# The head of a mixer reordered: x times its norm early, adaLN sums as columns on TensorE, h^T written ahead of the filter norms

## The chip, the cores and the metric

One of the cores of a Trainium2 chip runs the whole program. The metric is the device time of one execution in microseconds (us). The kernel before has a median of 2262.38 us over 3 runs (2261.64 to 2263.37). One more execution was taken by the hardware profiler; the views quoted here are of that one.

The engines are called as in the profile: PE (TensorE, matmul) with PEld (its weight loads), DVE (VectorE), ACT (ScalarE), POOL (GpSimd), SP (the queue that issues most DMAs).

## The reference, cut to what matters

The program is one encoder block on x (1024 tokens of 1024 channels, float32): a mixer (a Hyena branch with long convolutions, and attention) and 16 experts. What the change touches is the beginning of the mixer:

```python
h = RMSNorm(x)*(1+scale1)+shift1        # scale1, shift1: columns of silu(c) @ w_ada + b_ada
z = h @ w_in                            # 34 blocks of 128 columns

# the filters of the Hyena branch
hdn = jnp.sin(fr[0] * (z @ w1 + b1))
hdn = jnp.sin(fr[1] * (hdn @ w2 + b2))
hdn = jnp.sin(fr[2] * (hdn @ w3 + b3))
h = (hdn @ w4).reshape(L, HY_ORDER, 2, HY_WIDTH)
h = h * jnp.exp(-t01[:, :, None, None] * jnp.abs(deltas))
h = h / (jnp.sum(jnp.abs(h), axis=0, keepdims=True) + EPS)
```

In the filter part z is a table of time features, and h is the filters; in the first two lines h is the normed x. w_ada gives six groups of 1024 columns; the head needs the first two, the shift and the scale.

## The kernel before, in words

Nearly all products are made to float32 accuracy from three matmuls of split operands (`mm3`, L143 to L146: high by high, high by low, low by high). An operand is split by a copy to a shorter format on ACT and a subtraction on DVE (`wsplit`, L136; the `wl` and `wh` tiles). A projection block of w_in is 1024 by 128, its tile `wr` of 512 KB comes from a ring of two buffers (`wload`, L131).

The program is `mixer_head`, then `attention`, `merge`, `project`, `choose`, `experts`. The change lies in `mixer_head`. It computes, for x transposed to channels by tokens (`xt`, eight tiles of 128 by 1024):

- the filter network: three layers of 66, 128 and 64 inputs (L237, L309), each followed by `sine` (range reduction on DVE, L223 to L229) and `sin` on ACT. The results, split, are `Hs`.
- the sum of x² over the channels: ACT squares a tile (L254), PE multiplies it with a column of ones (L256; row form: the ones are a one-column weight, the square moves 512 columns at a time, and all eight k add up in PSUM). `columns()` turns the row into columns by two ACT copies (L244) and eight one-column matmuls (L247). `rsqrt` (L148) makes r, eight transposes (L334) spread it over all partitions, and ACT copies that to `rb` (L335).
- the scale group of adaLN: of its eight weight tiles `stage[1][k]`, four are scaled on ACT (L315, L317) and added on POOL (L318), four more are accumulated by `adaln` on DVE (L157 to L162) into `acc`, and `mod_cols` (L164) sums over the partitions with eight one-column matmuls (L167). G1 is (1 + scale) times the norm's gain.
- the shift group: row form on PE (L342, `stage[0][k]` moving 512 columns at a time), then `columns()`.
- h^T: DVE makes x times G1 times rb (L349), ACT adds the shift and rounds to `hTh` (L358), DVE makes the rest `hTl` (L359).
- the filter norms: `norms(o)`, o = 0 and 1, is a generator. Each multiplies split w4 with `Hs` (L271, L272), takes Abs on ACT (L274), multiplies with the decay (L266) and sums on DVE (L275), eight times; then it scales w4 by 1/norm. Four steps of norms(0) stand in front of h^T, the rest behind it, then norms(1).

Behind that come: the spectra of the filters (a plane of filter values is made by `filt_plane`, L415; its matmul is L420 and L421), transforms by `fft8` on DVE, the blocks 12 to 17 of w_in (q, k, v), the blocks 0 to 11 (Hyena's inputs), the two convolutions, and the blocks 18 to 33 (gates). The gates' blocks have the lowest priority (`lane(2)`): they fill PE where nothing else is ready.

A scheduler that works ahead of time fixes the order on each engine from the order of the program, priorities and its own estimates of time. Inside `in_order()` (L113) PE, ACT and DVE keep the written order among themselves; the head from the first sine to h^T stands in such a block. SP issues the DMAs in one sequence, and a DMA waits for the one issued eight before it.

Of the kernel before, what the change touches and what calls it, by code (L numbers as in the profile page):

```python
# [51 lines left out]
def block(tc, xT, cols_d, rows_d, mlp_d, w4_d, dfc_d, idf_d, rope_d, wada_d, win_d, why_d, watt_d, wout_d, wr_d,  # L52
          wg_d, wu_d, wd_d, out, dbg=None, upto=99):
    nc = tc.nc
# [127 lines left out]
    def mixer_head():  # L182
# [11 lines left out]
        def z4(shape=(128, 1024), dt=F32):  # L194
            return wk.tile(list(shape), dt, name="z4", tag="z4", bufs=3)
# [19 lines left out]
        nc.sync.dma_start(delb, row("del"))  # L215

# [20 lines left out]
            mm(ps, mcol(w, parts), h, start=True, stop=True)  # L237
            return ps

        def columns(row):  # L240

            t = z4([1, 1024])
            for hf in range(2):
                nc.scalar.copy(t[:, hf * 512:hf * 512 + 512], row[hf])  # L244
            ps = pM([128, 8])
# [4 lines left out]
        sums = [pT([1, 512]) for hf in range(2)]  # L250

        def square(k):
            sq = z4()
            nc.scalar.activation(sq, xt[k], AF.Square)  # L254
            for hf in range(2):
                mm(sums[hf], ones[:, 0:1], sq[:, hf * 512:hf * 512 + 512], start=k == 0, stop=k == 7)  # L256

        w4s = []

        def norms(o):  # L260
            raw = w4r[o]
            w4h, w4l = wsplit(raw)
            yield
            for b in range(4):
                dec = wk.tile([128, 1024], F32, name="dec", tag="Z", bufs=4)
                nc.scalar.activation(dec, t01b, AF.Exp, scale=col("ndel", b))  # L266
                for dr in range(2):
                    m = dr * 4 + b
                    ps = pS()
                    for hf in range(2):  # L270
                        mm(ps[:, hf], w4h[:, m * 128:(m + 1) * 128], Hs[hf], start=True, stop=False)  # L271
                        mm(ps[:, hf], w4l[:, m * 128:(m + 1) * 128], Hs[hf], start=False, stop=True)  # L272
                    t = f4([128, 1024])
                    nc.scalar.activation(t, ps.rearrange("p a b -> p (a b)"), AF.Abs)  # L274
                    nc.vector.scalar_tensor_tensor(t, t, 1.0, dec, op0=ALU.mult, op1=ALU.mult,  # L275
                                                   accum_out=rn[:, o * 8 + m:o * 8 + m + 1])
                    yield
# [15 lines left out]
        Hs = []  # L293
        with in_order():
            h = sine(layer("w1", mcol("z", 66), 66), "b1", "f1")
            for k in range(3):
                square(k)
            sin(h)
            ps = layer("w2", h)
            for k in range(3, 7):  # L300
                square(k)
            h = sine(ps, "b2", "f2")
            sin(h)
            square(7)
# [5 lines left out]
            n0 = norms(0)  # L310
            next(n0)
            hs = [sine(t, "b3", "f3") for t in ps]
            pv = columns(sums)
            acc, w = z4(), stage[1]
            nc.scalar.activation(acc, w[0], AF.Copy, scale=siluc[:, 0:1])  # L315
            for k in range(1, 4):
                nc.scalar.activation(w[k], w[k], AF.Copy, scale=siluc[:, k:k + 1])  # L317
                nc.gpsimd.tensor_add(acc, acc, w[k])  # L318
                if k > 1:
                    s = hs[k - 2]  # L320
                    sin(s)
                    t = hsp.tile([128, 512], F32R, name=f"Hs{len(Hs)}")
                    nc.scalar.copy(t, s)
                    nc.vector.tensor_sub(t[64:128], s[64:128], t[64:128])
                    Hs.append(t)
# [3 lines left out]
            rb = w2("H", [128, 1024])  # L329
            for hf in range(2):  # L330
                ps = pM()
                for j in range(4):
                    q = hf * 4 + j
                    nc.tensor.transpose(ps[:, j * 128:j * 128 + 128], rr[:, q:q + 1].to_broadcast([128, 128]), ident)  # L334
                nc.scalar.copy(rb[:, hf * 512:hf * 512 + 512], ps)  # L335
            for k in range(4, 8):
                adaln(acc, w[k], k)
            prow = [pT([1, 512]) for hf in range(2)]

            def shift(k):  # L340
                for hf in range(2):
                    mm(prow[hf], siluc[:, k:k + 1], stage[0][k][:, hf * 512:hf * 512 + 512], start=k == 0, stop=k == 7)  # L342
            for k in range(4):
                next(n0)
                shift(k)
            mod_cols(acc, 1, pM)
            nc.vector.scalar_tensor_tensor(G1, modc[:, 8:16], 1.0, col("g_mix", 0, 8), op0=ALU.add, op1=ALU.mult)
            for k in range(8):
                nc.vector.scalar_tensor_tensor(xt[k], xt[k], G1[:, k:k + 1], rb, op0=ALU.mult, op1=ALU.mult)  # L349
                if k < 4:  # L350
                    shift(k + 4)
            nc.vector.tensor_add(modc[:, 0:8], columns(prow), col("b_ada", 0, 8))
            sx.close()
            hpool = hx.enter_context(tc.tile_pool(name="hT", bufs=1, side="right", reuse_waits="tile"))
            hTh, hTl = [[hpool.tile([128, 1024], F32R, name=f"hT{i}{k}") for k in range(8)] for i in range(2)]
            for k in range(8):
                u, b = xt[k], modc[:, k:k + 1]
                nc.scalar.activation(hTh[k], u, AF.Identity, bias=b)  # L358
                nc.vector.scalar_tensor_tensor(hTl[k], u, b, hTh[k], op0=ALU.add, op1=ALU.subtract)  # L359
        for _ in n0:  # L360
            pass
        if "Hs" in dbg:
            for hf in range(2):
                nc.sync.dma_start(dbg["Hs"][hf], Hs[hf].bitcast(F32))
# [2 lines left out]
                nc.sync.dma_start(dbg["hT"][0, k], hTh[k].bitcast(F32))  # L367
                nc.sync.dma_start(dbg["hT"][1, k], hTl[k].bitcast(F32))

        for _ in norms(1):  # L370
            pass


        def win_block(m, evac, n=0):
            raw = wload(win_d[m])
            wh, wl = wsplit(raw)
            for hf in range(2):
                sl = slice(hf * 512, hf * 512 + 512)
                ps = pM()
                with lane(n) if n else ExitStack():  # L380
                    for k in range(8):
                        ks = slice(k * 128, k * 128 + 128)
                        mm3(ps, (wh[:, ks], wl[:, ks]), (hTh[k][:, sl], hTl[k][:, sl]), k == 0, k == 7)
                evac(ps, sl)

        def hyena_in(m, n=0):
# [1054 lines left out]
```

## Time and profile before

| | us |
|---|---|
| median of 3 runs | 2262.38 |
| lowest, highest | 2261.64, 2263.37 |
| the profiled execution | 2259.1 |
| its span on the core | 2257.3 |
| PE busy, of the span | 2126.8 (94%) |
| DVE busy | 1905.6 (84%) |
| ACT busy | 1310.2 (58%) |
| POOL busy | 126.3 (6%) |

How to read the views: times count from the start of the span. A windows row gives a stretch (from:to and its length), the busy time and count of instructions of PE, PEld, DVE, ACT and POOL, then PEclk (the clock that TensorE was granted, 1.00 is full), the share of the DMA engines and GB/s. A timeline row is start, length, engine, line, operation, output tile and inputs, partitions x elements, how many instructions in a row; in brackets the idle time ahead of it and what ended it. A group's row is line, engine, operation, tiles, count, then busy time in us and mean ns of one, then idle time before and its releasers. A matmul of float32 operands is carried out as more than one pass and leaves more than one record.

### The profile page before, as it was taken

Reading aid. Unit: us, or ns where it says so; the run is one execution under the profiler, and the core shown is the slowest. Engines: PE = TensorE matmul, PEld = TensorE weight load, DVE = VectorE, ACT = ScalarE, POOL = GpSimd, SP = SyncE. Lnnn points to the kernel's source line nnn. Section 1 sums busy time; section 2 is a strip of 40 time slices with the busy share of each in tenths; the row PEclk is TensorE's granted clock in tenths of the full one; section 3 lists DMA queues with packets and bytes.
Section 4 is the critical chain, followed back from the end, with each engine's and each line's share of the span. In section 5 each row is a group of like instructions: output and inputs, shape, how many; then the busy total and the mean of one; then the engine's idle time right before and its main releaser. Section 6 shows DMA issues by size and latency. Waiting matters only on the chain. (4 is left out here: it accounts for less than half of the span.)

```text
span 2257.3 us, 26834 instructions
## 1 busy us (share of the span) xinstructions
PE 2126.8 (94%) x10076; PEld 1682.6 (75%) x10076; DVE 1905.6 (84%) x2150; ACT 1310.2 (58%) x1424; POOL 126.3 (6%) x130
## 2 busy tenths in 40 slices
PE   5799999999979999998699999999999999999997
PEld 1487887878768887775577777777778777787776
DVE  6888897998968888644789988898998989889986
ACT  5654453242367774213477766677677677677675
POOL 1011000010000000002100010000000000000000
PEclk8899999999989999998899999999999999999999
DMA  7046755554442224667699999999999999999984
GB/s 281 21 142 201 289 205 168 172 155 153 144 145 94 66 66 143 212 226 278 222 361 369 364 363 321 377 368 375 363 355 377 371 375 360 359 377 365 380 323 149
DMA packets 138134, 588.87 MB, mean 261 GB/s; under 512 B 13714, under 2 KB 34450, under 8 KB 88724
## 3 DMA queue, kind: packets, MB, share of 16 engines
q1 hardware_dynamic: 122308, 546.25, 64.6%
q0 software_dynamic: 15696, 40.90, 7.0%
q8 instruction: 79, 1.29, 0.2%
q14 instruction: 51, 0.42, 0.1%
HBM read 530.48 MB, written 56.62 MB: 260 GB/s over the span
## 5 line engine op out<-in xcount | busy, mean ns | idle before, releaser
L1161 DVE TENSOR_TENSOR el<-raw,eh 128x2048 fp32r<-128x2048 f32 (+1 forms) x451 | 861.6, 1947 | 61.2 <-ACT eh L1160 58.5
L1160 ACT CAST eh<-raw 128x2048 fp32r<-128x2048 f32 (+1 forms) x456 | 721.6, 1642 | 58.2 <-PE py L146 29.8
L145 PE MATMUL pM<-el,xh 128*128 128x512 f32 x1024 | 405.4, 396 | 8.7 <-DVE el L1161 8.6
L144 PE MATMUL pM<-eh,xh 128*128 128x512 f32 x1024 | 405.8, 396 | 7.9 <-ACT eh L1160 6.1
L146 PE MATMUL pM<-eh,xl 128*128 128x512 f32 x1024 | 400.9, 392 | 0.0
L145 PEld LDWEIGHTS pM<-el,xh 128*128 128x128 f32 x1024 | 192.3, 188 | 62.0 <-DVE el L1161 24.1
L144 PEld LDWEIGHTS pM<-eh,xh 128*128 128x128 f32 x1024 | 192.2, 188 | 50.3 <-ACT eh L1160 8.9
L146 PEld LDWEIGHTS pM<-eh,xl 128*128 128x128 f32 x1024 | 192.3, 188 | 37.7
L144 PE MATMUL pM<-hT,wh 128*128 128x512 f32 x544 | 214.2, 394 | 4.8 <-ACT wh L139 3.7
L146 PE MATMUL pM<-hT,wl 128*128 128x512 f32 x544 | 212.9, 392 | 0.6 <-DVE wl L140 0.6
L145 PE MATMUL pM<-hT,wh 128*128 128x512 f32 x544 | 213.2, 392 | 0.0
L145 PE MATMUL py<-el,hh 128*128 128x512 f32 x512 | 205.2, 401 | 1.4 <-DVE el L1161 1.3
L144 PE MATMUL py<-eh,hh 128*128 128x512 f32 x512 | 201.8, 394 | 1.8 <-ACT hh L1236 1.5
L146 PE MATMUL py<-eh,hl 128*128 128x512 f32 x512 | 200.6, 392 | 0.0
L139 ACT CAST wh<-wr 128x1024 fp32r<-128x1024 f32 (+1 forms) x60 | 56.2, 936 | 162.5 <-PE pM L145 83.4
L144 PEld LDWEIGHTS pM<-hT,wh 128*128 128x128 f32 x544 | 102.6, 189 | 26.1 <-ACT wh L139 4.1
L146 PEld LDWEIGHTS pM<-hT,wl 128*128 128x128 f32 x544 | 102.3, 188 | 22.2 <-DVE wl L140 1.3
L145 PEld LDWEIGHTS pM<-hT,wh 128*128 128x128 f32 x544 | 102.6, 189 | 20.9
L144 PEld LDWEIGHTS py<-eh,hh 128*128 128x128 f32 x512 | 96.5, 188 | 26.2 <-ACT hh L1236 6.0
L145 PEld LDWEIGHTS py<-el,hh 128*128 128x128 f32 x512 | 96.4, 188 | 24.0 <-DVE el L1161 4.7
L146 PEld LDWEIGHTS py<-eh,hl 128*128 128x128 f32 x512 | 96.6, 189 | 19.1 <-DVE hl L1237 0.4
L1224 ACT ACTIVATE hd<-pM 128x512 f32<-128x512 f32 x64 | 38.3, 598 | 113.2 <-PE pM L146 113.0
(368 smaller groups left out, 3467.2 us busy)
## 6 DMA issues: line engine op xcount, KB each, us to landing
raw<-in_wg_dram SPq DMA_DIRECT2D x128, 1024.0 KB, 7.1
raw<-in_wu_dram SPq DMA_DIRECT2D x128, 1024.0 KB, 6.9
raw<-in_wd_dram SPq DMA_DIRECT2D x128, 1024.0 KB, 7.4
wr<-in_win_dram SPq DMA_DIRECT2D x34, 512.0 KB, 3.7
dc<-in_dfc_dram POOLq DMA_DIRECT2D x48, 256.0 KB, 2.9
wr<-in_wada_dram SPq DMA_DIRECT2D x24, 512.0 KB, 3.8
st<-in_wada_dram SPq DMA_DIRECT2D x16, 512.0 KB, 10.0
H<-H_s SPq DMA_DIRECT2D x16, 512.0 KB, 3.8
```

Of the source, the lines that this page charges most:

```text
L139: nc.scalar.copy(h, raw)
L144: mm(o, a[0], b[0], start=start, stop=False)
L145: mm(o, a[0], b[1], start=False, stop=False)
L146: mm(o, a[1], b[0], start=False, stop=stop)
L1160: nc.scalar.copy(h[:, ks], raw[:, ks])
L1161: eng.tensor_sub(l[:, ks], raw[:, ks], h[:, ks])
L1224: nc.scalar.activation(hd, ps2[0], AF.Silu)
```

## The change

- Order of the loads: before mlp, x, w4[0], t01, scale weights, w4[1], shift weights, del. After: mlp, x, scale weights, shift weights, the block 12 of w_in, w4[0], t01, w4[1], del. The w4 tiles leave the ring `wr` for buffers of their own.
- x²: the first two squares are summed by column groups (`by_columns`: the tile's eight 128 by 128 pieces are the weights, a column of ones moves), the other six are added on DVE into `total`, which is then summed by one group into the same eight PSUM columns. `columns()` goes.
- rb stays in PSUM, and x is multiplied by it at once, between the steps of `adaln` on the first four scale tiles.
- The scale: `acc` (four tiles, DVE) by a column group, and four more groups with the other tiles as weights and silu(c) as the moving column. No ACT scaling, no POOL addition.
- The shift: eight column groups instead of the row form.
- h^T: x times G1 plus shift, on ACT for odd k and on DVE for even k; a cast on ACT gives `hTh`, a subtraction on DVE `hTl`.
- `norms` is a plain function now; both calls stand behind h^T, outside the block that keeps the written order.
- The block 12 of w_in is loaded and split in the head, and its two halves run together, k by k.

```diff
-        w4r = [wload(w4_d[0])]
+        for i in (1, 0):
+            for k in range(8):
+                nc.sync.dma_start(stage[i][k], wada_d[i, k])
+        first = wload(win_d[12])
+        w4r = [w2("X", [128, 1024]) for o in range(2)]
+        nc.sync.dma_start(w4r[0], w4_d[0])
         t01b = w2("H", [128, 1024])
         nc.sync.dma_start(t01b, row("t01"))
-        for k in range(8):
-            nc.sync.dma_start(stage[1][k], wada_d[1, k])
-        w4r.append(wload(w4_d[1]))
-        for k in range(8):
-            nc.sync.dma_start(stage[0][k], wada_d[0, k])
+        nc.sync.dma_start(w4r[1], w4_d[1])
...
-        def columns(row):
...
+        def by_columns(ps, w, v, start, stop):
+
             for m in range(8):
-                mm(ps[:, m:m + 1], t[:, m * 128:(m + 1) * 128], ones[0:1, 0:1], start=True, stop=True)
-            return ps
+                mm(ps[:, m:m + 1], w[:, m * 128:(m + 1) * 128], v, start=start and m == 0, stop=stop and m == 7,
+                   skip_group_check=True)
...
             h = sine(layer("w1", mcol("z", 66), 66), "b1", "f1")
-            for k in range(3):
-                square(k)
+            pv = pT([128, 8])
+            for k in range(2):
+                by_columns(pv, square(k), ones[:, 0:1], k == 0, False)
             sin(h)
             ps = layer("w2", h)
-            for k in range(3, 7):
-                square(k)
+            total = zt()
+            nc.vector.tensor_add(total, square(2), square(3))
             h = sine(ps, "b2", "f2")
+            sq = square(4)
+            nc.vector.tensor_add(total, total, sq)
             sin(h)
...
+            for k in range(5, 8):
+                nc.vector.tensor_add(total, total, square(k))
+            by_columns(pv, total, ones[:, 0:1], False, True)
...
-            acc, w = z4(), stage[1]
-            nc.scalar.activation(acc, w[0], AF.Copy, scale=siluc[:, 0:1])
-            for k in range(1, 4):
-                nc.scalar.activation(w[k], w[k], AF.Copy, scale=siluc[:, k:k + 1])
-                nc.gpsimd.tensor_add(acc, acc, w[k])
...
+            acc = zt()
+            for k in range(4):
+                adaln(acc, stage[1][k], k)
+                for i in (2 * k, 2 * k + 1):
+                    nc.vector.tensor_mul(xt[i], xt[i], rb.rearrange("p a b -> p (a b)"))
+            pg = pM([128, 8])
+            by_columns(pg, acc, ones[:, 0:1], True, False)
+            for k in range(4, 8):
+                by_columns(pg, stage[1][k], siluc[:, k:k + 1], False, k == 7)
...
-            for k in range(4):
-                next(n0)
-                shift(k)
-            mod_cols(acc, 1, pM)
...
+            pg = pM([128, 8])
             for k in range(8):
-                nc.vector.scalar_tensor_tensor(xt[k], xt[k], G1[:, k:k + 1], rb, op0=ALU.mult, op1=ALU.mult)
-                if k < 4:
-                    shift(k + 4)
-            nc.vector.tensor_add(modc[:, 0:8], columns(prow), col("b_ada", 0, 8))
+                by_columns(pg, stage[0][k], siluc[:, k:k + 1], k == 0, k == 7)
+            first = wsplit(first)
+            nc.vector.tensor_add(modc[:, 0:8], pg, col("b_ada", 0, 8))
...
-            for k in range(8):
-                u, b = xt[k], modc[:, k:k + 1]
-                nc.scalar.activation(hTh[k], u, AF.Identity, bias=b)
-                nc.vector.scalar_tensor_tensor(hTl[k], u, b, hTh[k], op0=ALU.add, op1=ALU.subtract)
-        for _ in n0:
-            pass
+
+            def shifted(k):
+                if k % 2:
+                    nc.scalar.activation(xt[k], xt[k], AF.Identity, scale=G1[:, k:k + 1], bias=modc[:, k:k + 1])
+                else:
+                    nc.vector.tensor_scalar(xt[k], xt[k], G1[:, k:k + 1], modc[:, k:k + 1], op0=ALU.mult, op1=ALU.add)
+
+            shifted(0)
+            for k in range(0, 8, 2):
+                nc.scalar.copy(hTh[k], xt[k])
...
+        norms(0)
...
-        for _ in norms(1):
-            pass
+        norms(1)
```

What this does to the order on the engines. PE before, at the end of the adaLN sums: the last column group of the scale (`z_262` is acc), the last rows of the shift (`st_106` to `st_109` are the weights' tiles), and the turn into columns:

```order
L167 MATMUL pM<-ones,z_262 128x1 [waits DVE_49]
L167 MATMUL pM<-ones,z_262 128x1 x7
L342 MATMUL pT<-st_106,siluc 1x512 [waits DMAHW1_49]
L342 MATMUL pT<-st_106,siluc 1x512
L342 MATMUL pT<-st_107,siluc 1x512 [waits DMAHW2_49]
L342 MATMUL pT<-st_107,siluc 1x512
L342 MATMUL pT<-st_108,siluc 1x512 [waits DMAHW3_49]
L342 MATMUL pT<-st_108,siluc 1x512
L342 MATMUL pT<-st_109,siluc 1x512 [waits DMAHW4_49]
L342 MATMUL pT<-st_109,siluc 1x512
L247 MATMUL pM<-ones,z_375 128x1 [waits Activation_49]
L247 MATMUL pM<-ones,z_375 128x1 x3
```

PE after, at the end of the same sums: the last two of the eight shift groups, and then the filter norms' first matmuls (`z_455` and `z_456` are the split w4, `Hs_333` and `Hs_335` the network's result):

```order
L244 MATMUL pM<-siluc,st_108 128x1 [waits DMAHW0_49]
L244 MATMUL pM<-siluc,st_108 128x1 x7
L244 MATMUL pM<-siluc,st_109 128x1 [waits DMAHW1_49]
L244 MATMUL pM<-siluc,st_109 128x1 x7
L269 MATMUL pS<-Hs_333,z_455 128x512 [waits DVE_49,Activation_49]
L270 MATMUL pS<-Hs_333,z_456 128x512
L269 MATMUL pS<-Hs_333,z_455 128x512 [waits PE_49]
L269 MATMUL pS<-Hs_335,z_455 128x512 [waits DVE_49]
L270 MATMUL pS<-Hs_335,z_456 128x512
L270 MATMUL pS<-Hs_333,z_456 128x512
L269 MATMUL pS<-Hs_335,z_455 128x512
L270 MATMUL pS<-Hs_335,z_456 128x512
```

The sums that were matmuls of 512 moving columns are matmuls of one moving column now, eight for each weight tile, and no norm matmul stands between them any more.

ACT before, where h^T begins (`f_126` to `f_128` are x's tiles, `f_343` and `f_431` the norms'):

```order
L423 ACTIVATE wn<-delb,cols 128x512 [waits DMAHW5_49]
L274 ACTIVATE f_343<-pS 128x1024 [waits DVE_49,PE_49]
L244 COPY z_375<-pT 1x512 [waits PE_49] x2
L274 ACTIVATE f_431<-pS 128x1024 [waits DVE_49,PE_49]
L358 ACTIVATE hT_392<-f_126,modc 128x1024 [waits DVE_49]
L358 ACTIVATE hT_393<-f_127,modc 128x1024 [waits DMAHW6_49]
L358 ACTIVATE hT_394<-f_128,modc 128x1024 [waits DMAHW7_49]
```

ACT after, at the same place (`f_466` and `f_474` are the norms', `X` the raw w4):

```order
L264 ACTIVATE dec<-H,cols 128x1024 [waits DVE_49,PE_49]
L272 ACTIVATE f_466<-pS 128x1024 [waits PE_49]
L260 CAST z_549<-X 128x1024 [waits DMAHW5_49]
L357 CAST hT_415<-f_126 128x1024 [waits DVE_49]
L351 ACTIVATE f_127<-f_127,modc,G_73 128x1024
L272 ACTIVATE f_474<-pS 128x1024 [waits DVE_49,PE_49]
L359 CAST hT_416<-f_127 128x1024 [waits Activation_49]
L357 CAST hT_417<-f_128 128x1024
```

Since the norms stand outside the block that keeps the written order, the scheduler has put the first Abs and the second w4's cast ahead of h^T's first cast, and twelve norm matmuls ahead of the first projection matmul on PE.

More of the change, by code (lines that the diff above doesn't have):

```diff
@@ L254, in square, with zt @@
             nc.scalar.activation(sq, xt[k], AF.Square)
-            for hf in range(2):
-                mm(sums[hf], ones[:, 0:1], sq[:, hf * 512:hf * 512 + 512], start=k == 0, stop=k == 7)
+            return sq
+        def zt(dt=F32):
+            return wk.tile([128, 1024], dt, name="zt", tag="Z", bufs=4)
         w4s = []
@@ L261, in norms @@
             raw = w4r[o]
-            w4h, w4l = wsplit(raw)
-            yield
+            w4h, w4l = z4(dt=F32R), z4(dt=F32R)
+            nc.scalar.copy(w4h, raw)
+            nc.vector.tensor_sub(w4l, raw, w4h)
             for b in range(4):
@@ L309, in mixer_head @@
                 mm(ps[hf], mcol("w3")[pr], h[pr], start=True, stop=True)
-            n0 = norms(0)
-            next(n0)
-            hs = [sine(t, "b3", "f3") for t in ps]
-            pv = columns(sums)
-            acc, w = z4(), stage[1]
-            nc.scalar.activation(acc, w[0], AF.Copy, scale=siluc[:, 0:1])
-            for k in range(1, 4):
-                nc.scalar.activation(w[k], w[k], AF.Copy, scale=siluc[:, k:k + 1])
-                nc.gpsimd.tensor_add(acc, acc, w[k])
[L319 to L325, printed above, removed]
+            for k in range(5, 8):
+                nc.vector.tensor_add(total, total, square(k))
+            by_columns(pv, total, ones[:, 0:1], False, True)
+            h = [sine(ps[0], "b3", "f3")]
             v, rr, rt = v1, r1, rt1
@@ L340, in shift @@
-            def shift(k):
-                for hf in range(2):
-                    mm(prow[hf], siluc[:, k:k + 1], stage[0][k][:, hf * 512:hf * 512 + 512], start=k == 0, stop=k == 7)
-            for k in range(4):
-                next(n0)
-                shift(k)
-            mod_cols(acc, 1, pM)
+            rb = pS()
+            for q in range(8):
+                nc.tensor.transpose(rb[:, q // 4, q % 4 * 128:q % 4 * 128 + 128],
+                                    rr[:, q:q + 1].to_broadcast([128, 128]), ident)
@@ new lines, in mixer_head @@
+            h.append(sine(ps[1], "b3", "f3"))
+            for t in h:
+                sin(t)
+            acc = zt()
[7 more added lines that the diff above has]
+                by_columns(pg, stage[1][k], siluc[:, k:k + 1], False, k == 7)
@@ L347, in mixer_head @@
+            for hf in range(2):
+                t = hsp.tile([128, 512], F32R, name=f"Hs{hf}")
+                nc.scalar.copy(t, h[hf])
+                Hs.append(t)
+            nc.vector.tensor_add(modc[:, 8:16], pg, col("b_ada", 8, 8))
             nc.vector.scalar_tensor_tensor(G1, modc[:, 8:16], 1.0, col("g_mix", 0, 8), op0=ALU.add, op1=ALU.mult)
+            for hf in range(2):
+                nc.vector.tensor_sub(Hs[hf][64:128], h[hf][64:128], Hs[hf][64:128])
+            pg = pM([128, 8])
@@ L368, in mixer_head, with step @@
                 nc.sync.dma_start(dbg["hT"][1, k], hTl[k].bitcast(F32))
-        for _ in norms(1):
-            pass
+        norms(1)
         def win_block(m, evac, n=0):
[L375 to L378, printed above, removed]
+            wh, wl = first if m == 12 else wsplit(wload(win_d[m]))
+            def step(ps, sl, k):
+                ks = slice(k * 128, k * 128 + 128)
+                mm3(ps, (wh[:, ks], wl[:, ks]), (hTh[k][:, sl], hTl[k][:, sl]), k == 0, k == 7)
+            halves = [slice(hf * 512, hf * 512 + 512) for hf in range(2)]
+            if m == 12:
+                ps = [pM() for sl in halves]
+                for k in range(8):
+                    for hf, sl in enumerate(halves):
+                        step(ps[hf], sl, k)
+                for hf, sl in enumerate(halves):
+                    evac(ps[hf], sl)
+                return
+            for sl in halves:
                 ps = pM()
```

25 lines of the change are left out of this document (7 added, 18 removed).

## The prediction

> **What bounds the kernel now.** I read the page's totals first, then busy time by stage, then PE's waits, then the timeline at the seams.
>
> ```profile
> span 2257.3 us, 26834 instructions
> PE 2126.8 (94%) x10076; PEld 1682.6 (75%) x10076; DVE 1905.6 (84%) x2150; ACT 1310.2 (58%) x1424; POOL 126.3 (6%) x130
> ```
>
> The windows view (busy us per engine, PEclk the granted clock) cuts the span where the head ends and where attention's tail begins:
>
> ```profile
> 12.41:43.00 30.59, 16.43 (x51) 4.74 (x49) 20.49 (x23) 15.24 (x19) 7.80 (x3) 0.78 0.97 394
> 43.00:108.00 65.00, 47.10 (x161) 26.06 (x162) 52.07 (x74) 41.10 (x45) 0.00 (x0) 0.82 0.05 17
> 108.00:370.00 262.00, 258.11 (x1179) 209.29 (x1178) 223.72 (x320) 130.30 (x187) 19.66 (x37) 1.00 0.61 203
> 370.00:607.00 237.00, 232.05 (x1042) 189.27 (x1040) 221.33 (x275) 72.93 (x94) 11.15 (x22) 1.00 0.48 149
> ```
>
> From 108 to 607 PE is busy 490.2 of 499 us: it is the bound there, and DVE has 38 and 16 us to spare in the two stages. So the head (0 to 108) is a prologue in front of a PE-bound stretch. It costs what passes until the first filter plane can be multiplied, less whatever matmuls of the projections PE gets done before, for those are missing from the stretch behind. Two times mark it: the first ACTIVATE of h^T and the first filter plane.
>
> ```profile
> 73.38 8.41 ACT L358 ACTIVATE hT<-f,modc 128x1024 fp32r<-128x1024 f32 x8
> ...
> 107.40 0.63 PE L420 MATMUL pT<-w4h,Hs 128*128 128x512 f32 x1
> ```
>
> The head's waits on PE name the chain to the first of them (us in total, times, longest):
>
> ```profile
> PE pM L334 <- DVE r L155: 15.9, 1, 15.9
> ...
> PE pS L271 <- ACT f L274: 10.8, 5, 8.0
> ```
>
> DMA doesn't bind it: it has little left to move after 40 us (DMA share 0.14 here, 0.05 above), and PE does nothing in the 10 us before.
>
> ```profile
> 30.00:40.00 10.00, 0.00 (x0) 0.00 (x0) 9.72 (x10) 2.30 (x3) 5.68 (x3) 0.50 1.02 419
> 40.00:50.00 10.00, 4.24 (x13) 2.85 (x14) 8.41 (x14) 6.49 (x9) 0.67 (x1) 0.50 0.14 49
> ```
>
> **The clock.** The granted clock decides this case, so I looked for what moves it. All its changes in this trace lie on one grid of 3.413 us. Windows on that grid, with PE's busy time and the clock:
>
> ```profile
> 60.20:63.61 3.41, 3.41 (x21) 2.20 (x21) 2.02 (x5) 0.00 (x0) 0.00 (x0) 1.00 0.00 0
> 94.33:97.75 3.42, 1.99 (x8) 1.36 (x8) 3.42 (x7) 3.42 (x5) 0.00 (x0) 1.00 0.39 134
> 101.16:104.57 3.41, 2.40 (x5) 1.47 (x6) 3.31 (x7) 0.40 (x1) 0.00 (x0) 0.50 0.00 0
> 104.57:107.99 3.42, 3.42 (x13) 3.03 (x13) 1.38 (x2) 0.43 (x1) 0.00 (x0) 0.50 0.46 158
> 1043.25:1046.66 3.41, 3.41 (x23) 2.29 (x22) 0.27 (x2) 2.19 (x4) 0.00 (x0) 1.00 0.01 2
> 1046.66:1050.07 3.41, 2.73 (x15) 2.00 (x14) 1.66 (x9) 2.33 (x4) 0.00 (x0) 0.50 0.00 0
> ```
>
> 94.33 holds only 1.99 us of 512-column matmuls, and the next window keeps 1.00. 1043.25 is busy all of its 3.41 us, and the clock falls. What fills it are matmuls that move one column:
>
> ```profile
> 1043.49 1.05 PE L974 MATMUL pT<-ones,sq 128*128 128x1 f32 x8
> ...
> 1045.43 1.05 PE L974 MATMUL pT<-ones,sq 128*128 128x1 f32 x8
> ```
>
> I take it that a one-column matmul counts for next to nothing as activity. The window at 60.20, just over half columns and the rest 512-column, kept its clock, so the threshold lies between its wide share (0.44) and the other's (a third). To rise it takes more: 2.40 us of wide matmuls (101.16) did not do it, a full window (104.57) did.
>
> The Trainium skill ("TensorE: Matmul & The Clock Gate", "Part 1: The HAM clock gate") lets the clock rise after about one busy window of 3.4 us; by it the new chain would be warm almost at once, and the time that of the first rival below. The trace's 1043.25, busy throughout and followed by 0.50, disagrees.
>
> **The price of a column group** (8 matmuls, 16 records). At full clock, L167's group takes 16 loads in 1.86 us, and PE follows the loads:
>
> ```profile
> 60.23 1.95 PE L167 MATMUL pM<-ones,z 128*128 128x1 f32 x16
> 60.23 1.86 PEld L167 LDWEIGHTS pM<-ones,z 128*128 128x128 f32 x16 [0.86 <-issue]
> 47.28 0.34 PEld L271 LDWEIGHTS pS<-Hs,wh 128*128 128x128 f32 x1
> 51.44 0.19 PEld L271 LDWEIGHTS pS<-Hs,wh 128*128 128x128 f32 x1 [0.86 <-issue]
> ```
>
> One load takes 0.34 us at clock 0.50 (47.28) and 0.19 at 1.00 (51.44). So a group is 1.86 us warm and 1.86 x 0.34/0.19 = 3.3 us cold.
>
> The same page, "LDWEIGHTS (loading the stationary operand)", gives a load by its columns alone, P/1.2 ns, with no clock in it; by that a group's 16 loads would be some 1.7 us at either clock (an estimate from that page), the second rival. The rows with 0.34 and 0.19 disagree.
>
> **The change, in order of time.** The new head gives PE no wide matmul but the filter layers until h^T, so I run its PE at half clock throughout.
>
> Its prices, from the timeline (start, us, engine, line, operation) and, for Square and the scalings, from the groups of the head (busy us, mean ns):
>
> ```profile
> 4.57 2.08 PE L237 MATMUL pM<-f 66*128 66x512 f32 x2 [4.57 <-DMA f<-in_mlp_dram]
> ...
> 6.68 0.81 DVE L223 TENSOR_SCALAR wf<-pM,cols 128x512 f32<-128x512 f32 x1 [5.61 <-PE pM L237]
> ...
> 8.45 2.14 DVE L228 SCALAR_TENSOR_TENSOR wf<-sl,wf 128x512 f32<-128x512 f32 x3
> 10.63 0.43 DVE L229 TENSOR_SCALAR wf<-wf 128x512 f32<-128x512 f32 x1
> ...
> 28.62 6.30 DVE L228 SCALAR_TENSOR_TENSOR wf<-sl,wf 128x512 f32<-128x512 f32 x3
> ...
> 45.76 1.94 PE L334 MATMUL pM<-ident,r 128*128 128x128 f32 x8 [15.94 <-DVE r L155]
> ...
> 47.88 3.92 DVE L162 SCALAR_TENSOR_TENSOR z<-st,siluc,z 128x1024 f32<-128x1024 f32 x3
> ```
>
> ```profile
> L275 DVE SCALAR_TENSOR_TENSOR f<-f,dec 128x1024 f32<-128x1024 f32 x16 | 18.9, 1224 | 6.0 <-ACT f L274 5.3 <-ACT dec L266 0.7
> ...
> L254 ACT ACTIVATE z<-f 128x1024 f32<-128x1024 f32 x8 | 8.4, 1056 | 9.2 <-DMA f<-in_xT_dram 6.5 <-PE pT L256 2.7
> ```
>
> x²: the first two squares become column groups, from 9.1 us (first layer, sine and Square before) to 9.1 + 6.6 = 15.7; layer 2 to 17.8 (2.08 cold); its sine to 22.2 (from before's first sine: its three L228 in 2.14, L229 0.43 and three steps ahead of them, 6.68 to 11.06, 4.4). The six other squares are summed on DVE; of those five adds, four lie behind the sine at 1.2 each (the price of L275, the same width): 27.2. ACT's Squares at 1.06 keep ahead. The total's group ends at 30.5. Third sine meanwhile, then v and the Newton steps to 33.2, transposes of the norm 1.94, to 35.2. Before, they ended at 47.7: x's norm is ready 12 us earlier. Part of that is the removed POOL adds: three of L228 take 2.14 us alone, 6.30 beside them.
>
> Then DVE: fourth sine to 37.6; four adaLN steps (3.92 for three, about 1 for the first) and, of the x scalings at 1.22, the six ahead of the last step: 4.9 + 7.3 = 12.2, acc ready at about 50. All weights have landed by then, so the DMA's new order costs nothing; what moved behind it (w4, t01, del) is needed only later.
>
> PE: thirteen column groups in one chain (acc, four of the scale, eight of the shift), each waiting for nothing else: 13 x 3.3 = 43 us, to 93. The shift's row form (L342) goes away. h^T then starts at 93 against 73.4: **20 us later**. x is already scaled, so h^T itself is no longer than before.
>
> Behind that ACT is the longest: by the order, five norm matmuls still stand between the chain and the first Abs (at twice the warm 0.23 of the pair below, 2.3 us). The groups of the head:
>
> ```profile
> L274 ACT ACTIVATE f<-pS 128x1024 f32<-128x1024 f32 x16 | 16.1, 1019 | 7.2 <-PE pS L272 5.9 <-DVE f L275 1.4
> ...
> L342 PE MATMUL pT<-st,siluc 128*1 128x512 f32 x32 | 14.8, 601 | 0.0
> ...
> L266 ACT ACTIVATE dec<-H,cols 128x1024 f32<-128x1024 f32 x8 | 9.0, 1148 | 0.0
> ```
>
> One pair of the projections' matmuls in the timeline:
>
> ```profile
> 109.65 0.40 PE L145 MATMUL pM<-hT,wh 128*128 128x512 f32 x1
> 109.88 0.40 PE L146 MATMUL pM<-hT,wl 128*128 128x512 f32 x1
> ```
>
> L342's 14.8 us, which go, lay partly beside DVE's work on x; what they cost is already in before's 73.4. From the first Abs to the first plane ACT has 16 Abs, eight casts of h^T, four shifts, the decays not yet made (four) and five casts of weights: 37 items at about 1.0, 37 us; with 3 us of stalls (PE cold, transposes of the norms) the first plane comes at 93 + 2.3 + 40 = 135, **28 us later** than 107.4. "h^T ahead of the filter norms" isn't quite done: one Abs and one cast stand ahead of the first cast of h^T; this lies in the sum.
>
> Given back: by the order PE now has 93 projection matmuls done ahead of the first plane, before it had 7. At the pitch of 0.23 us (109.65 to 109.88) 86 of them are 19.8 us that are missing behind 108, where PE is the bound.
>
> Sum: 28 - 19.8 = +8 us. Further on the order uses the projections up earlier (all done ahead of the last 28 token transposes, before of the last 16), so some filler is missing at the end of the PE-bound stretch; I add 1. 2259.1 (the profiled execution, span 2257.3) + 9 = 2268.1; the three runs' median, 2262.38, lies 3.3 above the profiled time: 2271.4, so **2272**. The unknown costs: the column group between 2.9 and 3.6 (5 us either way over 13), stalls between 0 and 8: 2264 to 2280.
>
> **The rivals.**
> First, faster: columns count as activity, the chain warms within one window of its start. 13 x 1.86 + 1.7 = 26 us, h^T at 76, first plane at 76 + 1.2 + 40 = 117, +10; minus 19.8: -10, 2252. Deciding point: a group under 2.6 us (3.3 less 9/13) makes the sum negative. For it: 60.20 kept its clock; against it: 1043.25. Chance 0.13.
> Second: loads cost the same at either clock. 13 x 1.9 = 25, plane at 50 + 25 + 2.3 + 40 = 117, so 2252 to 2257 with what stays cold. Against it: 0.34 and 0.19. Chance 0.05.
> Third, slower still: DVE becomes the bound in the mixer. It has 38 us to spare from 108 to 370, and starts its transforms 28 us late with filler already spent; if half of the 19.8 us done ahead come back as PE's waits for planes, that is 10 more, 2282. For it: DVE is busy 223.7 of 262; against: it has 16 more later. Chance 0.08.
>
> **How the numbers follow.** The forecast has 0.74. Some 0.2% (4.5 us) is what a measurement of this kernel can tell. Faster than 2257.9: first rival 0.12, second 0.03, the forecast's tail 0.01: 0.16. Within: the rest of both rivals 0.03, the forecast's low end (a group at 2.9) 0.11: 0.14. Slower: 0.70. The range 2258 to 2286 leaves out the fast rivals, 0.16, and a little above, 0.03. The forecast's own is 2264 to 2280.
>
> **What would show it.** Right: granted clock 0.50 from about 13 to about 95 us; L244's thirteen groups at 3.2 to 3.4 us; first h^T cast near 93; first plane near 135; PE past 98% from there to the tail. Wrong: groups at 1.9 us or the clock at 1.00 in the chain (first rival), loads at 0.19 with the clock at 0.50 (second), PE waits for DVE's spectra after 140 us (third); an acc that is ready much before 50 would move everything earlier.

## The result and the profile after

The changed kernel takes 2291.54 us (median of 4 runs, 2288.93 to 2292.72) against 2262.88 (4 runs, 2261.64 to 2265.99): 1.0123 times as long, 95% interval 1.0105 to 1.0141. It is slower by 28.7 us, not by the 9.6 that were forecast, and lies above the range. The profiled execution's span is 2290.4, 33.1 more than before. One of the ten executions of e3_less_pe, below, took 5902.09 us, and its ratio is that of the other nine.

The head and PE-bound stretch in the windows view of the profile after:

```profile
0.00:50.00 50.00, 18.57 (x64) 13.39 (x64) 34.38 (x51) 22.26 (x25) 2.56 (x9) 1.00 0.87 338
50.00:95.00 45.00, 44.59 (x209) 44.59 (x210) 6.54 (x10) 1.15 (x1) 0.00 (x0) 1.00 0.04 12
95.00:140.00 45.00, 42.16 (x173) 31.60 (x173) 38.23 (x58) 37.62 (x40) 0.00 (x0) 1.00 0.11 41
140.00:639.00 499.00, 481.15 (x2146) 386.69 (x2146) 446.70 (x595) 201.06 (x280) 31.66 (x60) 0.99 0.53 175
```

From 50 to 95 PE does one thing, and DVE and ACT have next to nothing to do (6.54 and 1.15 of 45 us). The timeline shows what it is, and what it leads to:

```profile
50.41 3.57 PE L244 MATMUL pM<-ones,zt 128*128 128x1 f32 x16 [13.28 <-DVE zt L162]
53.84 8.46 PE L244 MATMUL pM<-siluc,st 128*128 128x1 f32 x39
```

```profile
97.32 1.02 ACT L272 ACTIVATE f<-pS 128x1024 f32<-128x1024 f32 x1 [42.16 <-PE pS L270]
98.24 1.04 ACT L260 CAST z<-X 128x1024 fp32r<-128x1024 f32 x1
99.17 1.04 ACT L357 CAST hT<-f 128x1024 fp32r<-128x1024 f32 x1
```

```profile
140.04 0.50 PE L433 MATMUL pT<-w4h,Hs 128*128 128x512 f32 x1
```

The thirteen column groups begin at 50.41, and the first norm matmul behind them at 94.80. h^T's first cast comes at 99.17 (before 73.38), the first filter plane at 140.04 (before 107.40). Their price stands in the groups of that stretch (busy us, mean ns of one):

```profile
L244 PEld LDWEIGHTS pM<-siluc,st 128*128 128x128 f32 x192 | 41.1, 333 | 0.0
```

A load of 0.33 us is one at half clock (0.34 at 47.28 in the trace of before, where 0.50 is on record). The windows show 1.00 there because the clock's first recorded change in this trace is its rise at 100.33, and ahead of it the column has no value to show. So the half clock is read from the loads, about 0.33 us each up to 99.42 and 0.19 from 101.53 on, not from PEclk.

Some of this delay belongs to the one execution that was profiled. In it the network's input lands at 5.74 (before 4.57) and the first column group begins at 10.56. In the traces of e9_after_less_dve and e10_after_less_pe, whose heads are the same, that group begins at 7.99 and near 8.2, acc's group at 47.85 and 48.03 instead of 50.41, and the first plane comes at 137.5 and 137.6. Between traces, a difference of 2.5 us in these times says nothing.

Behind the first plane, PE is busy 481.15 of 499 us, 10 less than in 107 to 607 before:

```profile
107.00:607.00 500.00, 491.17 (x2221) 399.37 (x2219) 445.52 (x594) 203.67 (x281) 30.80 (x59) 1.00 0.54 177
```

But the stretch is no shorter. Three markers show where it ends: the last gate (ACTIVATE of `ge`), the last token transposes (`wf`) and attention's first exponential (`P`). A row by line gives count, durations in ns (shortest, median, longest), and the first and last start. Three rows of before, then three of after:

```profile
L714 ACT ACTIVATE ge<-pM,cols x32: 673/688/695, 401.2 to 607.3; 128x512 f32<-128x512 f32 x32
```

```profile
L671 PE MATMUL pT<-ident,wf x32: 270/273/329, 601.9 to 622.4; 128*128 128x128 f32 x32
```

```profile
L781 ACT ACTIVATE P<-pS,rs x64: 1110/1120/1135, 638.6 to 866.6; 128x1024 f32<-128x1024 f32 x64
```

```profile
L727 ACT ACTIVATE ge<-pM,cols x32: 672/687/692, 420.7 to 620.7; 128x512 f32<-128x512 f32 x32
```

```profile
L684 PE MATMUL pT<-ident,wf x32: 272/273/477, 628.8 to 651.1; 128*128 128x128 f32 x32
```

```profile
L794 ACT ACTIVATE P<-pS,rs x64: 1110/1118/1127, 668.7 to 896.5; 128x1024 f32<-128x1024 f32 x64
```

The plane is 32.6 us late, the last gate 13.4, the last token transpose 28.7, P 30.1. From the first plane to P it takes 531.2 us before and 528.7 after. PE has done 93 projection matmuls ahead of the plane instead of 7, just as the order said, and 2.5 us come back, where 19.8 were forecast. The windows from the first plane to P, before and after:

```profile
107.40:638.65 531.25, 504.07 (x2282) 408.09 (x2280) 462.54 (x616) 215.20 (x297) 34.49 (x65) 0.99 0.56 184
```

```profile
140.04:668.70 528.66, 493.99 (x2196) 394.75 (x2195) 460.86 (x614) 209.82 (x291) 34.30 (x65) 0.98 0.55 180
```

PE has 86 matmul records fewer to do there (2196 instead of 2282). It is busy 10.1 us less, but it stands idle 34.7 us instead of 27.2.

### The profile page after: what moved, and what is told of

Its sections match the earlier page's. It is cut to its first block, busy times and chain, and to the rows that moved or that the text cites. A ratio compares the mean times of both kernels' runs of the same rounds, so it can differ in the third digit from the quotient of the medians.

```text
span 2290.4 us, 27131 instructions
## 1 busy us (share of the span) xinstructions
PE 2157.1 (94%) x10220; PEld 1729.8 (76%) x10220; DVE 1906.1 (83%) x2159; ACT 1304.8 (57%) x1419; POOL 117.8 (5%) x127
```

## The experiments

Theory T: the head ends late because thirteen groups of one-column matmuls run at half clock, and its delay reaches the end in full. Each run has its own runs of before beside it; differences in us below are the ratio's distance from 1, times 2262, so that the changed kernel stands at +27.8.

### The clock: e2_prewarm

```diff
+            warm = pM([1, 512])
+            for k in range(12):
+                mm(warm, siluc[:, 0:1], stage[1][4 + k % 4][:, 0:512], start=True, stop=True)
             pg = pM([128, 8])
             by_columns(pg, acc, ones[:, 0:1], True, False)
```

> The changed kernel with 12 more matmuls of 512 moving columns (their result is not used) in PE's idle time ahead of acc's group, 24 records of about 0.9 us at half clock, so that the chain of column groups starts at full clock. Theory T (a one-column matmul counts for nothing as activity): the clock falls back to 0.50 within one or two windows of 3.4 us, the thirteen groups take 41 to 45 us; time within 4 us of the changed kernel or up to 10 more, if the burst itself ends behind acc. Rival (columns keep a warm clock, they only could not raise it): the groups take 1.86 each, the chain 25 us, h^T 19 us earlier, about 2272.

Measured: 2286.55 us (2 runs), ratio 1.0111 (1.0089 to 1.0134). The windows on the clock's grid:

```profile
35.27:38.68 3.41, 3.41 (x6) 0.50 (x6) 3.31 (x6) 1.03 (x2) 0.00 (x0) 1.00 1.03 420
38.68:42.10 3.42, 3.42 (x10) 0.66 (x9) 3.42 (x4) 3.37 (x5) 0.00 (x0) 1.00 1.02 415
42.10:45.51 3.41, 3.41 (x9) 0.67 (x8) 3.41 (x4) 3.40 (x4) 0.00 (x0) 1.00 0.54 194
45.51:48.93 3.42, 2.21 (x8) 0.56 (x6) 3.42 (x4) 0.37 (x1) 0.00 (x0) 1.00 0.00 0
48.93:52.34 3.41, 3.41 (x33) 3.41 (x32) 1.90 (x2) 1.15 (x1) 0.00 (x0) 1.00 0.00 0
52.34:55.75 3.41, 3.41 (x19) 3.41 (x18) 0.00 (x0) 0.00 (x0) 0.00 (x0) 0.50 0.00 0
55.75:89.70 33.95, 33.95 (x161) 33.95 (x161) 3.91 (x6) 0.00 (x0) 0.00 (x0) 0.50 0.05 16
```

The burst of wide matmuls raises the clock at 38.68; that is the first change on record here, so the 1.00 of the first row is no reading, and its 6 matmuls against 10 in the next row show the half clock. The first window that holds columns and nothing else, 48.93 to 52.34, is busy throughout (33 matmuls, against 19 in the next), and at its end the clock falls and stays down for 37 us of a PE that never pauses. The time is 2.7 us under the changed kernel's, as T has it. So the rival, that columns keep a full clock, is out, and with it the faster case of the prediction. The first group of the chain still ran at full clock; its loads took 1.86 us:

```profile
48.62 1.86 PEld L244 LDWEIGHTS pM<-ones,zt 128*128 128x128 f32 x16 [2.15 <-DVE zt L162]
```

This also speaks to the Trainium skill ("TensorE: Matmul & The Clock Gate", "Part 1: The HAM clock gate"), by which PE gets its full clock after about one busy window. This trace disagrees, if busy means what it means in the profile: the 33.95 us from 55.75 to 89.70, all of them busy, did not raise it. What is counted instead is not shown; only that wide matmuls raised the clock here, and one-column matmuls did not.

### One part alone on the kernel before: e8_shift_columns

```diff
-                for hf in range(2):
-                    mm(prow[hf], siluc[:, k:k + 1], stage[0][k][:, hf * 512:hf * 512 + 512], start=k == 0, stop=k == 7)
+                for m in range(8):
+                    mm(pcol[:, m:m + 1], stage[0][k][:, m * 128:(m + 1) * 128], siluc[:, k:k + 1],
+                       start=k == 0 and m == 0, stop=k == 7 and m == 7, skip_group_check=True)
...
```

The turn of the row into columns goes with it.

> The kernel before with one part of the change: the shift's sums as eight column groups in the place of the row form, in the same order between the same norm matmuls. Theory T (columns let the clock fall, and the end follows the head): the clock at 0.50 for most of 53 to 85, the eight groups over 20 us instead of 14.8, h^T's first cast 5 to 10 us later, time 4 to 10 us more than before. Rival (columns cost no more than rows as long as norm matmuls stand between them, and save the turn of the row): h^T's first cast 2 to 4 us earlier, time 0 to 4 us less.

Measured: 2272.77 us (4 runs), ratio 1.0052 (1.0035 to 1.0069), +11.8.

```profile
49.23:52.64 3.41, 3.41 (x28) 3.23 (x27) 2.96 (x4) 2.05 (x3) 0.00 (x0) 1.00 0.03 7
52.64:56.06 3.42, 3.42 (x14) 3.03 (x13) 1.23 (x2) 2.92 (x4) 0.00 (x0) 0.50 0.00 0
56.06:86.77 30.71, 30.54 (x127) 28.43 (x126) 15.22 (x20) 7.10 (x8) 0.00 (x0) 0.50 0.00 1
```

Even with four norm matmuls (0.9 us) between two groups (2.2 and 2.4 us) the clock falls after one window, and it stays down to 86.77. h^T's first tile moved from 73.4 to 84.1, the plane from 107.4 to 118.2, with 7 projection matmuls ahead of it as before. The form of the sum alone delays the head in the way T says, and the end with it; the time is 1.8 above the 4 to 10 that I gave it.

### The start of the chain: e1_acc_last

```diff
-            pg = pM([128, 8])
-            by_columns(pg, acc, ones[:, 0:1], True, False)
...
+            pg = pM([128, 8])
+            for k in range(4, 8):
+                by_columns(pg, stage[1][k], siluc[:, k:k + 1], k == 4, False)
+            pb = pM([128, 8])
+            for k in range(8):
+                by_columns(pb, stage[0][k], siluc[:, k:k + 1], k == 0, k == 7)
             acc = zt()
...
+            by_columns(pg, acc, ones[:, 0:1], False, True)
```

> The changed kernel with the twelve column groups that need only the loads put ahead of acc's group, which stays last (it waited 13.3 us for DVE at the head of the chain). Theory T (the head's delay reaches the end of the program in full, since the stretch behind the first filter plane is bound by its own chain and not by PE): the groups run at half clock from 37 to 78, acc's group ends at 82, h^T's first cast at 85 instead of 99, the first plane at 127 instead of 140; 13 us less than the changed kernel, about 2278. Rival R (PE's amount of work bounds the stretch, as predicted): the matmuls done ahead stay the same 93, so the same 13 us; but if PE's amount of work decided alone, with PE no less idle in all, the time would move by less than 5, 2287 to 2292.

Measured: 2276.8 us (4 runs), ratio 1.0066 (1.0049 to 1.0082), +14.9, 12.9 less than the changed kernel.

```profile
34.99 40.96 PE L244 MATMUL pM<-siluc,st 128*128 128x1 f32 x192
75.81 3.55 PE L244 MATMUL pM<-ones,zt 128*128 128x1 f32 x16
```

The groups ran from 34.99 to 79.4, h^T's cast came at 84.6, the plane at 125.5: 14.5 us earlier than in the trace of the changed kernel, some 12 earlier than in those of e9 and e10. The matmuls done ahead stayed at 93. Nearly one for one, as T has it; the less than 5 that R gave is out.

### What bounds the stretch: five cuts

e3_less_pe takes PE work away from the kernel before: it leaves out the last of the eight k in the sums of the gate blocks. e4_less_dve takes DVE work away: it leaves out two of the four products of each spectrum multiplication. e5_both_less leaves out both. e9_after_less_dve and e10_after_less_pe do e4's and e3's cut to the changed kernel. The edit of e3, then that of e4:

```diff
-                    for k in range(8):
+                    last = 6 if n == 2 else 7
+                    for k in range(last + 1):
...
```

```diff
-            W = f4()
-            nc.vector.tensor_mul(W[:, 0], t[:, 1], H[:, 1])
-            nc.vector.tensor_mul(W[:, 1], t[:, 0], H[:, 1])
             nc.vector.tensor_mul(t, t, H[:, 0:1, :].to_broadcast([128, 2, 512]))
-            nc.vector.tensor_sub(t[:, 0], t[:, 0], W[:, 0])
-            nc.vector.tensor_add(t[:, 1], t[:, 1], W[:, 1])
+            nc.vector.tensor_sub(t[:, 0], t[:, 0], H[:, 1])
+            nc.vector.tensor_add(t[:, 1], t[:, 1], H[:, 1])
```

> The kernel before, with the last of the eight k left out in the 16 gate blocks of the projection (96 matmuls of 0.23 us, 22 us of PE work at the lowest priority; the gates' sums are incomplete). Theory T (the stretch from 108 to 607 is bound by the chain through DVE, and PE is 98% busy only because the gates fill it): 2255 to 2262, at most 7 us less. Rival R (PE's amount of work bounds it, the step 'given back' of the prediction): 20 to 22 us less, 2241 to 2243.

> The kernel before, with two of the four half-width products of each spectrum multiplication left out (16 calls of two DVE instructions of 0.69 us, 22 us of DVE work in the convolutions; the product with the filters' spectra is wrong). Theory T (the chain through DVE bounds the stretch): 12 to 22 us less, 2241 to 2251. Rival R (PE bounds it): within 4 us of before, PE's busy time being the same.

Measured: e3 2262.89 us (10 runs), ratio 1.0012 (1.0002 to 1.0022); e4 2262.61 (10 runs), 1.0008 (0.9999 to 1.0018). Neither cut gains anything. The first half of T's claim holds (PE's amount of work does not decide alone), the second falls: DVE's does not either. The markers say why. Gates, token transposes and P of e3, then of e4:

```profile
L715 ACT ACTIVATE ge<-pM,cols x32: 672/683/692, 399.3 to 576.0; 128x512 f32<-128x512 f32 x32
```

```profile
L672 PE MATMUL pT<-ident,wf x32: 272/273/473, 599.1 to 621.0; 128*128 128x128 f32 x32
```

```profile
L782 ACT ACTIVATE P<-pS,rs x64: 1112/1119/1125, 636.4 to 864.7; 128x1024 f32<-128x1024 f32 x64
```

```profile
L711 ACT ACTIVATE ge<-pM,cols x32: 674/688/693, 400.4 to 618.3; 128x512 f32<-128x512 f32 x32
```

```profile
L668 PE MATMUL pT<-ident,wf x32: 272/273/329, 581.4 to 603.4; 128*128 128x128 f32 x32
```

```profile
L778 ACT ACTIVATE P<-pS,rs x64: 1110/1120/1125, 636.5 to 865.0; 128x1024 f32<-128x1024 f32 x64
```

With less PE work the gates end 31 us earlier, and the transposes within 1.5 us of where they were. With less DVE work the transposes end 19 us earlier, but PE runs on with gates until 11 us later, and P comes behind the last gate. P starts at 636.4 and 636.5, 2 us from its 638.6 before. So I formed T2: two chains of equal length, PE's whole work and the chain of transforms through DVE, end together in the kernel before. A gain needs both to be shortened; a loss needs only one to be delayed.

> The kernel before with both cuts of e3_less_pe and e4_less_dve (the last k of the 16 gate blocks, and two of four products of each spectrum multiplication, left out). Each alone changed nothing: without the PE work the token transposes still ended at 621, without the DVE work they ended 19 us earlier but the gates' matmuls ran on to 619. Theory T2 (two chains of equal length end together, PE's work and the chain through DVE; a gain needs both): 15 to 20 us less than before, 2240 to 2247. Rival L (neither; a chain of latencies or the loads behind it sets the end): within 4 us of before.

Measured: 2242.65 us (4 runs), ratio 0.9911 (0.9890 to 0.9932): 20 us less, where each cut alone brought none. P's row:

```profile
L779 ACT ACTIVATE P<-pS,rs x64: 1110/1119/1125, 623.2 to 852.0; 128x1024 f32<-128x1024 f32 x64
```

> The changed kernel with the cut of e4_less_dve (two of four products of each spectrum multiplication left out, 22 us of DVE work in the convolutions). Theory T2 (two chains, PE's work and the chain through DVE; in the changed kernel PE's work ends 30 us ahead of the other, gates at 621, token transposes at 651): 15 to 20 us less than the changed kernel, 2271 to 2277, where the same cut brought the kernel before nothing. Rival R (PE's amount of work bounds it here too): within 4 us of the changed kernel.

Measured: 2274.87 us (4 runs), ratio 1.0062 (1.0045 to 1.0079), +14.0: 13.8 less than the changed kernel, a little under the 15 that T2 gave as the least. P starts at 652.5 instead of 668.7, and now the gates end last:

```profile
L724 ACT ACTIVATE ge<-pM,cols x32: 676/688/693, 419.3 to 634.1; 128x512 f32<-128x512 f32 x32
```

> The changed kernel with the cut of e3_less_pe (the last k of the 16 gate blocks left out, 22 us of PE work). Theory T2: within 4 us of the changed kernel, 2287 to 2295, the 20 us of matmuls done ahead being worth nothing for the same reason. Rival R: 18 to 22 us less, 2270 to 2274.

Measured: 2285.63 us (4 runs), ratio 1.0114 (1.0094 to 1.0134), +25.8: by the ratios 2.0 less than the changed kernel, within the intervals, and far from R's 18.

DVE's cut, worth nothing before, is worth 14 us after, and PE's is worth nothing in either. That is what the change did to the balance: it moved the plane, and with it the chain through DVE, some 30 us back, and PE's work 20 us forward.

### The sums as rows: e6_rows and e7_norms_first

```diff
+            pb = [pT([1, 512]) for hf in range(2)]
+            for k in range(8):
+                in_rows(pb, siluc[:, k:k + 1], stage[0][k], k == 0, k == 7)
+            pr = [pM([1, 512]) for hf in range(2)]
+            for k in range(4, 8):
+                in_rows(pr, siluc[:, k:k + 1], stage[1][k], k == 4, False)
+            pg = pS()[:, 0]
+            columns(pg[:, 8:16], pb)
             acc = zt()
...
-            by_columns(pg, acc, ones[:, 0:1], True, False)
-            for k in range(4, 8):
-                by_columns(pg, stage[1][k], siluc[:, k:k + 1], False, k == 7)
+            in_rows(pr, ones[:, 0:1], acc, False, True)
+            columns(pg[:, 0:8], pr)
```

> The changed kernel with the twelve sums over weight tiles, and acc's, in row form (one column of silu(c) or ones as the weights, 512 columns moving), ahead of acc, and two turns of a row into columns. Theory T (half clock and the late start cost the time; wide matmuls bring the clock up within two windows; the end follows the first plane one for one): the clock rises near 41, 48 records in 24 us, h^T's first cast at 68 to 72 instead of 99, the first plane at 109 to 113 instead of 140; 27 to 31 us less than the changed kernel, 2260 to 2266. Rival W (the time behind h^T is the matter: the norms placed behind it): h^T as early, but the first plane no earlier than 125, over 2272.

The twelve sums also stand ahead of acc here, as in e1_acc_last.

Measured: 2256.19 us (10 runs), ratio 0.9976 (0.9967 to 0.9986), -5.4: faster than both kernels. Its row sums in the timeline:

```profile
34.62 14.83 PE L249 MATMUL pT<-st,siluc 128*1 128x512 f32 x32
49.28 7.03 PE L249 MATMUL pM<-st,siluc 128*1 128x512 f32 x16
56.24 1.94 PE L257 MATMUL pS<-ones,ge 1*128 1x1 f32 x16
58.11 1.88 PE L249 MATMUL pM<-zt,ones 128*1 128x512 f32 x4
```

Twelve weight tiles take 21.6 us as rows (34.62 to 56.24), where twelve groups took 41.1. The clock rises at 36.53. At full clock twelve groups would take some 22 us too (an estimate: 12 times the 1.86 of e2_prewarm's first group), so by this what the rows save is the half clock. h^T's first cast comes at 66.6, the plane at 106.8, P at 635.5. T had the size about right, some 4 us too slow. With its sums as rows and ahead of acc, the change is worth about 5 us.

This run also weighs the matmuls done ahead by themselves: the plane comes where it came before (106.8 and 107.4), and 96 of them stand ahead of it instead of 7. By the prediction's pitch of 0.23 us that is 20.5 us; the time falls by 5.4.

e7_norms_first keeps the rows and puts norms(0) and the start of norms(1) between them, ahead of h^T.

```diff
                 in_rows(pb, siluc[:, k:k + 1], stage[0][k], k == 0, k == 7)
+                if k > 1:
+                    scaled(k - 2)
+                    next(n0)
...
                 in_rows(pr, siluc[:, k:k + 1], stage[1][k], k == 4, False)
+                if k < 6:
+                    scaled(k + 2)
+                next((n0, n0, n1, n1)[k - 4])
```

`scaled` is one scaling of x by its norm, with a step of acc ahead of every second. The run also copies rb out of PSUM and splits Hs earlier.

> e6_rows with the filter norms put back ahead of h^T: all of norms(0) and the start of norms(1) between the row sums, on an ACT and a DVE that are idle there. Theory T2 (the chain that ends late begins at the first filter plane, which needs norms(0) but not h^T; PE's work ends with it in before): the first plane at 80 to 90, h^T's first cast at 78 to 85, 10 to 22 us less than before, 2240 to 2252. Rival P (PE's own work then ends last, as it had only 7 us to spare): within 5 us of before, 2256 to 2266.

Measured: 2258.46 us (10 runs), ratio 0.9989 (0.9978 to 0.9999). The plane came at 110.0, not at 80 to 90, so this did not test T2, although the time fits rival P: the rest of norms(1) stands ahead of the first plane on ACT and DVE, and so does h^T, which began at 82.7.

### norms(1) behind the first spectra: e11 and e12

```diff
-        norms(1)
...
         spectra(0)
+        w4r.append(w2("X", [128, 1024]))
+        nc.sync.dma_start(w4r[1], w4_d[1])
+        norms(1)
         spectra(1)
```

This is e11's edit of e6_rows; e12 makes the same of e7_norms_first, with norms(0) alone ahead of h^T. In both the load of norms(1)'s w4 moves too.

> e6_rows with norms(1) and the load of its w4 moved behind the first filters' spectra, which need only norms(0). In e6_rows the gates end at 587 and the token transposes at 618, so PE has some 30 us to spare and the chain from the first plane decides. Theory T2: the first plane 14 to 18 us earlier than in e6_rows, near 90, but norms(1)'s work on DVE (8 sums of 1.22 and some 5 us more) now lies inside the chain: 2 to 12 us less than e6_rows, 2244 to 2254. Rival (what is moved into the chain costs as much there): 2253 to 2260.

> e7_norms_first (norms(0) ahead of h^T) with norms(1) and the load of its w4 behind the first filters' spectra. Theory T2: the first plane at 72 to 85, before h^T is done; the chain through DVE begins 20 us or more earlier than in e6_rows, PE's work as early as h^T allows (83): 2236 to 2250. Rival P (h^T, later and sharing ACT and DVE with the first transforms, then holds PE's work back): 2250 to 2260.

Measured: e11 2271.12 us (4 runs), ratio 1.0053 (1.0033 to 1.0073); e12 2271.4 (4 runs), 1.0044 (1.0027 to 1.0062). Both are slower than before, and both expectations and their rivals missed. The first plane did come early, at 92.5 and 76.1, but the last of them came later: 227.2 and 228.1, in e6_rows 210.1. Windows of e6_rows and of e11:

```profile
107.00:207.00 100.00, 99.67 (x431) 79.80 (x432) 87.47 (x115) 52.52 (x79) 14.26 (x27) 1.00 0.57 177
```

```profile
107.00:207.00 100.00, 99.72 (x435) 79.41 (x434) 79.09 (x107) 49.52 (x67) 9.97 (x19) 1.00 0.51 166
```

PE has no idle time in either, but in e11 DVE gets 8 us less to do in these 100. Where the planes stop is on record: e11's planes up to 185 and behind it, and between them the load that moved and its first use.

```profile
L446 PE MATMUL pT<-w4h,Hs x16: 389/390/502, 92.5 to 131.1; 128*128 128x512 f32 x16
```

```profile
160.43 0.32 SPq L545 DMA_DIRECT2D H_s<-f  x1
160.87 0.38 SPq L549 DMA_DIRECT2D X<-in_w_dram  x1
```

```profile
165.44 1.05 ACT L271 CAST z<-X 128x1024 fp32r<-128x1024 f32 x1 [2.96 <-DMA X<-in_w_dram]
```

```profile
L446 PE MATMUL pT<-w4h,Hs x16: 387/389/505, 185.3 to 227.2; 128*128 128x512 f32 x16
```

The first filter's planes end at 131.1. The load of norms(1)'s w4 is issued at 160.87, right behind the last store of the first spectra (160.43); norms(1) starts on it at 165.44, and the second filter's planes begin at 185.3, where e6_rows begins them at 149.9. e12 has the same gap (130.0 to 185.5). So the first plane marks the chain only where the other planes follow it without such a gap. How late norms with an early load would do, no run shows.

## Why the prediction was wrong, point by point

The whole head at half clock: right. e2_prewarm and e8_shift_columns show that columns do not hold the clock.

A group at 3.3 us: right; thirteen took 44.4 (50.41 to 94.80), 3.41 each. acc ready at about 50: 50.41, with some luck: two other executions of the same head had it at 47.9 and 48.0. (The 27.2 in the working of x² should be 27.1, which changes nothing.) h^T later by 20: 25.8 (73.38 to 99.17); the chain ended 2 us late, and h^T's first cast stands behind the Abs and the w4 cast (97.32, 98.24), which I had counted in the list behind it and not ahead of it.

First plane 28 us later, at 135: 32.6, at 140.04 (30.1 and 30.2 in e9 and e10). From the first Abs (97.32) to the plane it took 42.7 us, where 40 were forecast; the chain's late end is the other 2.

**The step that failed is "given back"**: 86 matmuls done ahead, 19.8 us "missing behind 108, where PE is the bound". They returned 2.5, and PE, which should have been past 98% behind the plane, was at 96.4% (481.15 of 499). I read the bound from PE's 490.2 busy of 499 us, and took DVE's 38 and 16 us of idle time for slack. But PE's busy time there is filled by gates with the lowest priority, which says that PE always had something to do, and not that the end waited for it. The two chains ended together (e3, e4, e5), and moving PE's work forward shortens only one of them:

| kernel | matmuls ahead of the plane | first plane | first P | between |
|---|---|---|---|---|
| before | 7 | 107.4 | 638.6 | 531.2 |
| e8_shift_columns | 7 | 118.2 | 651.6 | 533.4 |
| after | 93 | 140.0 | 668.7 | 528.7 |
| e1_acc_last | 93 | 125.5 | 654.0 | 528.5 |
| e6_rows | 96 | 106.8 | 635.5 | 528.7 |
| e7_norms_first | 73 | 110.0 | 637.7 | 527.7 |
| e5_both_less | 7 | 107.7 | 623.2 | 515.5 |

Over 33 us of difference in the plane and some 90 matmuls, the distance moves by less than 6 in these kernels, e5_both_less aside. It shortens where the chain that ends last is cut: in e5, and in e9 (137.5 to 652.5, 515.0). In e11 and e12 it is longer (553.4 and 571.6), with their gap between the planes.

The third rival, DVE as the bound of the mixer, came nearest to the mechanism. What ends late is the chain of planes and transforms through DVE, which itself is busy 460.86 of the 528.66 us from plane to P. The rival got a chance of 0.08 and half its price (10 us instead of 17). Without the 19.8 the prediction's own sum would have been 28 + 1 on 2262.4, near 2291, which is where the time came out. That this fits to the us is luck: the plane came 2 to 5 us later than forecast, and 2.5 came back. The first rival (columns keep the clock) is shown wrong by e2_prewarm, the second (loads cost the same at either clock) by the loads of 333 ns, against 0.19 us at full clock.

## What to carry to other kernels

An engine at 98% is the bound only if the last thing waited for is its work: with a filler of low priority it is busy in any case, so look at what ends last, the filler or the chain, before work that is done ahead is booked as time saved. Where two chains end together, a change that helps one and delays the other costs nearly the whole delay. To find out, shorten each alone and both together. And a long chain of one-column matmuls on TensorE ran at half clock here however dense it was: as rows, with 512 columns moving, the same twelve tiles took 21.6 us instead of 41.1.

## What the runs showed of the hardware

From full clock, one window of 3.41 us filled with one-column matmuls (48.93 to 52.34 in e2_prewarm) was enough to halve it, and some ten more windows of them did not bring it back (to 89.70). Mixed with wide ones, a window in which groups of 2 us alternate with 0.9 us of 512-column matmuls (49.23 in e8_shift_columns) lost the clock as well. The record of a weight load of 128 columns of float32 took 0.33 us at half clock (e2_prewarm from 55.75 on, clock 0.50 on record) and 0.19 at full (51.44 in before).
